# Conformer trunk: sixteen of one channel tile's 31 convolution taps on TensorE instead of all, and four small moves around them

## The chip, the cores and the metric

The kernel runs on one core of a Trainium2 chip. The metric is device time in microseconds (us) of one execution; lower is better. The engines of the core are TensorE (PE, matrix products), VectorE (DVE), ScalarE (ACT), GpSimd (POOL) and SyncE (SP, which issues loads). Each engine works through its own list of instructions in order and waits by semaphores for the others.

## The reference

`x` has 1024 tokens of 1024 channels. There are two layers; each has a token mixer and a SwiGLU feed-forward network of width 2816, both behind an RMS norm, a shift and scale from the conditioning vector `c`, and a gate. Layer 0 mixes tokens by a causal Conformer convolution, layer 1 by trailing means. The change touches the convolution of layer 0 and the norms around it:

```python
def conformer_conv(h, w1, b1, w_dw, b_dw, ln_g, ln_b, w2, b2):
    u = h @ w1 + b1                                # D -> 2D
    a, g = jnp.split(u, 2, axis=-1)
    u = a * jax.nn.sigmoid(g)
    u = lax.conv_general_dilated(                  # depthwise, causal, width 31
        u, w_dw[:, None, :].astype(u.dtype),
        window_strides=(1,), padding=[(CONV_WIDTH - 1, 0)],
        dimension_numbers=("NWC", "WIO", "NWC"),
        feature_group_count=D_MODEL) + b_dw
    u = jax.nn.silu(layer_norm(u, ln_g, ln_b))     # over channels
    return u @ w2 + b2

for i in range(DEPTH):
    mod = c_act @ ada_w[i] + ada_b[i]
    sh_m, sc_m, g_m, sh_f, sc_f, g_f = jnp.split(mod, N_ADA, axis=-1)
    h = modulate(rms_norm(x, norm_mix_g[i]), sh_m, sc_m)
    y = conformer_conv(h, ...) if i % 2 == 0 else multiscale_pool(h, ...)
    x = x + (1.0 + g_m)[:, None, :] * y
    h = modulate(rms_norm(x, norm_ffn_g[i]), sh_f, sc_f)
    y = swiglu_ffn(h, w_gate[i], w_up[i], w_down[i])
    x = x + (1.0 + g_f)[:, None, :] * y
return rms_norm(x, final_g)
```

## The kernel before

**Tiling.** Channels lie on the 128 partitions, so 1024 channels are eight channel tiles (`KT` = 8). Tokens lie along the free dimension in two chunks of 512, A (tokens 0 to 511) and B (512 to 1023). Every operand of a product is split into a high and a low part, and each product of 128x128 by 128x512 is done as three matmuls: high by high, low by high, high by low (`products`, L409). The profile names the high part `hhi`, `uhi`, `vhi` and the low part `hlo`, `ulo`, `vlo`.

**Weights.** `load_weight` (L394) brings a weight tile to `raw` by a DMA on SP's queue. ACT casts it to the high part and writes the negated high part beside it, and a DMA issued from POOL's queue (L403) adds the weight to that, which leaves the low part. Five weight tiles (`W_BUFS`) and three raw ones are in flight.

**Order.** PE's order is the program's own: `units` is a list of pieces of PE work (L1041 to L1077 for this stage), and `run_units` emits them in turn. The work of the other engines is a set of generators, the tasks. `pace` (L178) lets the tasks take steps while the model clock of PE advances, and gives each step to VectorE or GpSimd by their model clocks; `finish` (L190) drives a task to its end. Every matmul goes through one helper and shows as L122, every operation of DVE, ACT and POOL as L100; groups are told apart by their tiles.

**The stage of the change**, in PE's order:

1. `conv_in((A, p))` (L570) for tiles 4 and 5, then 6 and 7 together with B's 6 and 7: for each tile 24 matmuls for `a` and 24 for `g`; `conv_glu` (L562) has ACT take the sigmoid of `g` and DVE form `u`. `u` has 30 columns of halo in front. B's halo is A's last 30 columns, which GpSimd copies to `uhalo` (L568). The first four tiles of A were formed earlier.
2. In between stand the modulation steps: `ada_columns` (L352) loads 512 KB of `ada_w` per step (tile `adaw`, two buffers), PE multiplies it with `c` (group `ada`), and after every eight steps `columns_done` (L375) turns the result around on PE (`adac`), after which DVE adds the bias (`mod<-adac`). The unit `ada_first` starts this task. `norm_first` (L1045) is the task of B's first norm; its sum of squares is in `Squares` (L455): ACT squares a tile, DVE adds it.
3. Three tiles of B (0 to 2), then the taps. Seven of A's eight channel tiles are convolved by `Taps` (L633), whose 31 taps are shared one by one: DVE multiplies and adds into a spare PSUM bank (`ca`), or ACT multiplies (`pr`) and POOL adds (`pa`). At the end DVE adds `pa` to `ca` and does the last tap. Tile 7 is convolved on PE: `split_u` (L597) forms `uhi` and `ulo`, ACT makes a diagonal matrix per tap (`diagonals`, L604: 8 taps per weight buffer, a high and a low part each), and `pe_taps` (L614) runs 31 taps of three matmuls into one bank, `tap`, which ACT takes back to `u`.
4. Two more tiles of B, with the layer norm of A in between (`layer_norm_silu`, L703, a task): DVE sums the eight tiles into `acc` in SBUF, one add as each tile is finished; PE forms the mean over channels; the tiles are centred, squared and summed; PE forms `var` and `rstd`; silu; high and low parts `vhi` and `vlo`.
5. `conv_out` (L739): 192 products `y`. Then the last tile of B and the feed-forward network of A.

PSUM has six banks in turn for results of matmuls (`bank`, L238) and two spare ones for `ca`.

Of the kernel before, what the change touches and what calls it, by code (L numbers as in the profile page):

```python
# [9 lines left out]
F32 = mybir.dt.float32  # L10
F32R = mybir.dt.float32r
# [32 lines left out]

PE_TAPS = (7,)
DIAGS = 8
# [59 lines left out]
def trunk(ctx, tc, xT, c, vec, ada, adan, w1, w2, wgu, wdn, wpl, out):  # L106
# [348 lines left out]
    class Squares:  # L455


        def __init__(self, ch, psum=False):
            self.ch, self.acc, self.psum = ch, None, psum

        def add(self, k):
            ch = self.ch
            if self.acc is None:
                self.acc = bank("acc") if self.psum else temp(ch.n, "acc", 2)
                S_.activation(self.acc, x[ch.i][k], AF.Square)
            else:
                sq = temp(ch.n)
                S_.activation(sq, x[ch.i][k], AF.Square)
                was = self.acc
                if self.psum and k == KT - 1:  # L470
                    self.acc = temp(ch.n, "acc", 2)
                V_.tensor_tensor(self.acc, was, sq, op=ADD)

# [88 lines left out]
    def conv_glu(ch, p, ba, bg):  # L562
        u = st["u", ch.i, p]
        sg = temp(ch.n)
        S_.activation(sg, bg, AF.Sigmoid, bias=V("conv_b1", KT + p))
        V_.scalar_tensor_tensor(u[:, HALO:], ba, V("conv_b1", p), sg, op0=ADD, op1=MUL)
        if ch.i == 0:
            G_.tensor_copy(uhalo[:, p, :], u[:, ch.n : ch.n + HALO])  # L568

    def conv_in(*todo):  # L570

        def emit(take):
            got = {}
            for each in todo:
# [14 lines left out]
                conv_glu(ch, p, *b)  # L589
                if ch.i == 0 and p in PE_TAPS:  # L590
                    split_u(p)
                elif ch.i == 0:
                    T["taps", 0, p] = Taps(A, p)
        tiles = list(dict.fromkeys(e[1] for e in todo if e))
# [9 lines left out]
    def diagonals(p, js):  # L604

        def make():
            wt = wts.tile([P, 2, D], F32R, tag="w", name=nm("diag"))
            for i, j in enumerate(js):
                for part, w in enumerate((vecs[:, _COLS["conv_wdw"] + j * KT + p :][:, :1], wlow[:, j, p - PE_TAPS[0] : p - PE_TAPS[0] + 1])):
                    S_.activation(wt[:, part, i * P : i * P + P], ident, AF.Copy, scale=w)  # L610
            return wt
        return make

    def pe_taps(p):  # L614

        groups = [range(j, min(j + DIAGS, CW)) for j in range(0, CW, DIAGS)]
        us = []
        for i, js in enumerate(groups):
            def emit(take, i=i, js=js):
# [3 lines left out]
                for q, j in enumerate(js):  # L623
                    products(b, wt, q, [v[:, j : j + A.n] for v in st["us", p]], j == 0, j == CW - 1)
                    if q % 4 == 3:
                        pace()
                if i == len(groups) - 1:
                    S_.activation(st["u", 0, p][:, HALO:], b, AF.Identity, bias=V("conv_bdw", p))
                    st["taps", 0][p] = True
            us.append((emit, diagonals(p, js)))  # L630
        return us

    class Taps:  # L633
# [4 lines left out]

        def __init__(self, ch, p):
            self.ch, self.p, self.done, self.urgent = ch, p, False, False  # L640
            self.next, self.acc, self.part, self.busy = 0, None, None, 0
            tasks.append(self)

        def step(self, e):
# [6 lines left out]
            if self.next < CW - 1:  # L651
# [27 lines left out]
                return True  # L679
            if e != "V":  # L680
                return False
            if self.part is not None:
                V_.tensor_tensor(self.acc, self.part, self.acc, op=ADD)
# [313 lines left out]

    wdw = V("conv_wdw", 0, CW * KT).rearrange("p (j k) -> p j k", k=KT)[:, :, PE_TAPS[0] : PE_TAPS[-1] + 1]
    whigh = cst.tile([P, CW, len(PE_TAPS)], F32R, name="whigh")
    wlow = cst.tile([P, CW, len(PE_TAPS)], F32, name="wlow")  # L1000
    S_.copy(whigh, wdw)
# [171 lines left out]
```

## Time and profile before

| | |
|---|---|
| Median of three runs | 1880.17 us (1877.83 to 1882.66) |
| The profiled run | 1878.38 us, of which the span of the profile 1876.6 us |
| PE busy | 1821.7 us, 97% of the span |
| DVE, ACT, POOL busy | 971.8, 984.5, 622.2 us |
| Mean granted PE clock | 0.989 of full speed |
| DMA | 382.31 MB at 204 GB/s |

The times of single instructions, of stages and of waits come from the one profiled execution, the median from separate runs; the profiled run was 1.8 us below the median. In the tables of groups a row reads: line, engine, operation, out<-in, partitions x elements, count | busy time in us, mean ns of one | idle time of the engine just before them and who ended it. In order of time it reads: start, length, engine, line, operation, out<-in, count, and in brackets the idle time before.

### The profile page before, as it was taken

To read this page: it belongs to the slowest core of one execution; us is meant where nothing else is said; L and a number is where in the kernel's file an instruction comes from. 1 tells how busy PE (TensorE), PEld (TensorE's weight loads), DVE (VectorE), ACT (ScalarE), POOL (GpSimd) and SP (SyncE) were. 2 spreads that over 40 slices of the span, in tenths; PEclk is the share of its full clock that TensorE was granted. 3 is DMA by queue.
4 is the path that set the end of the run, shared out by engine and by line. 5 is a ranking of instruction groups with operands and counts; after the bars stand their busy time and mean duration, and the time that the engine had idled before them with its cause. 6 is when DMAs were issued, how large, how long until landed. Compare 5 with 4: busy or idle time off the path is not lost.

```text
span 1876.6 us, 22033 instructions
## 1 busy us (share of the span) xinstructions
PE 1821.7 (97%) x8197; PEld 1481.9 (79%) x8197; DVE 971.8 (52%) x1489; ACT 984.5 (52%) x1304; POOL 622.2 (33%) x668
## 2 busy tenths in 40 slices
PE   6899999999999999999999999999999999999996
PEld 4676678888888887888888888888888888888886
DVE  7699743998876235486533223644432233323225
ACT  3577756866756454554553445645534454443443
POOL 3488621787753211273211111421111111111111
PEclk9999989999999999999999999999999999999998
DMA  8968558899897986999887887878878879788882
GB/s 265 298 185 233 155 114 202 207 230 218 213 233 186 239 217 165 261 266 291 231 204 181 200 197 179 196 180 208 185 181 199 198 174 247 180 206 187 193 185 61
DMA packets 115292, 382.31 MB, mean 204 GB/s; under 512 B 11889, under 2 KB 22257, under 8 KB 115186
## 3 DMA queue, kind: packets, MB, share of 16 engines
q0 software_dynamic: 43488, 158.35, 46.2%
q1 hardware_dynamic: 70544, 221.51, 34.8%
q8 instruction: 64, 1.05, 0.2%
q10 hardware_dynamic: 1154, 1.05, 0.2%
q14 instruction: 42, 0.34, 0.0%
HBM read 376.67 MB, written 4.19 MB: 203 GB/s over the span
## 4 chain that ended last, share of the span: by engine, by line
PE 91%; DVE 4%; DMA 3%; ACT 0%; issue 0%; POOL 0%; SPq 0%; DVEq 0%; ACTq 0%; POOLq 0%
PE dn L122 25%; PE gate L122 25%; PE up L122 24%; PE y L122 6%; PE a L122 3%; PE g L122 3%; PE first L122 2%; DMA adaw<-in_adan_dram 2%; DVE t L100 1%; PE ada L122 1%; PE tap L122 1%; DVE x L100 1%; DVE adaw L100 1%; PE var L122 1%; DMA w<-in_wdn_dram 1%; DVE acc L100 1%
## 5 line engine op out<-in xcount | busy, mean ns | idle before, releaser
L100 ACT CAST w<-raw 128x1024 fp32r<-128x1024 f32 x312 | 326.0, 1045 | 514.8 <-issue 294.4
L122 PE MATMUL dn<-ghi,w 128*128 128x512 f32 (+1 forms) x1440 | 450.0, 389 | 2.2 <-ACT ghi L100 1.2
L122 PE MATMUL up<-hhi,w 128*128 128x512 f32 x1408 | 451.4, 390 | 0.0
L122 PE MATMUL gate<-hhi,w 128*128 128x512 f32 x1408 | 450.9, 390 | 0.0
L403 POOL DMA_DIRECT2D w<-in_wgu_dram x176 | 154.2, 876 | 767.6 <-ACT w L100 750.1
L100 DVE SCALAR_TENSOR_TENSOR x<-dn,gains,x 128x512 f32<-128x512 f32 (+1 forms) x360 | 261.8, 735 | 122.1 <-PE dn L122 121.7
L122 PEld LDWEIGHTS dn<-ghi,w 128*128 128x128 f32 x1440 | 270.4, 189 | 62.0 <-ACT ghi L100 1.6
L100 ACT ACTIVATE w<-raw 128x1024 fp32r<-128x1024 f32 x302 | 318.9, 1056 | 0.0
L100 DVE TENSOR_TENSOR t<-t,up 128x512 f32<-128x512 f32 x88 | 60.4, 686 | 492.4 <-PE up L122 472.0
L122 PEld LDWEIGHTS gate<-hhi,w 128*128 128x128 f32 x1408 | 264.3, 188 | 55.4
L122 PEld LDWEIGHTS up<-hhi,w 128*128 128x128 f32 x1408 | 264.3, 188 | 54.7
L122 PE MATMUL dn<-glo,w 128*128 128x512 f32 (+1 forms) x720 | 280.7, 390 | 1.6 <-POOL glo L100 1.6
L122 PE MATMUL gate<-hlo,w 128*128 128x512 f32 x704 | 274.3, 390 | 1.5 <-DVE hlo L100 1.5
L122 PE MATMUL up<-hlo,w 128*128 128x512 f32 x704 | 273.9, 389 | 0.0
L100 POOL TENSOR_TENSOR pa<-pa,pr 128x512 f32<-128x512 f32 x165 | 231.0, 1486 | 23.0 <-ACT pr L100 20.3
L100 DVE SCALAR_TENSOR_TENSOR ca<-u,vecs,ca 128x512 f32<-128x512 f32 x255 | 176.2, 746 | 0.7
L122 PEld LDWEIGHTS dn<-glo,w 128*128 128x128 f32 x720 | 136.6, 190 | 30.3 <-POOL glo L100 1.9
L122 PEld LDWEIGHTS gate<-hlo,w 128*128 128x128 f32 x704 | 132.1, 188 | 29.8 <-DVE hlo L100 2.3
L122 PEld LDWEIGHTS up<-hlo,w 128*128 128x128 f32 x704 | 132.2, 188 | 27.2
L403 POOL DMA_DIRECT2D w<-in_wdn_dram x88 | 77.9, 885 | 226.5 <-ACT w L100 224.4
L100 ACT ACTIVATE t<-gate 128x512 f32<-128x512 f32 x88 | 52.3, 594 | 161.0 <-PE gate L122 154.4
L100 DVE SCALAR_TENSOR_TENSOR adaw<-adaw,cact 128x1024 f32<-128x1024 f32 x64 | 106.2, 1660 | 36.0 <-DMA adaw<-in_ada_dram 35.8
(134 smaller groups left out, 1792.3 us busy)
## 6 DMA issues: line engine op xcount, KB each, us to landing
raw<-in_wgu_dram SPq DMA_DIRECT2D x176, 512.0 KB, 7.2
w<-in_wgu_dram POOLq DMA_DIRECT2D x176, 512.0 KB, 8.0
raw<-in_wdn_dram SPq DMA_DIRECT2D x88, 512.0 KB, 5.4
w<-in_wdn_dram POOLq DMA_DIRECT2D x88, 512.0 KB, 9.1
adaw<-in_ada_dram SPq DMA_DIRECT2D x48, 512.0 KB, 7.8
raw<-in_w_dram SPq DMA_DIRECT2D x44, 512.0 KB, 6.2
w<-in_w_dram POOLq DMA_DIRECT2D x34, 512.0 KB, 8.1
adaw<-in_adan_dram SPq DMA_DIRECT2D x32, 512.0 KB, 5.3
```

The source lines that it names most:

```text
L100: self.last = self.order(getattr(self.eng, name)(out, *args, **kw))
L122: last_mm[0] = nc.tensor.matmul(out, lhsT, rhs, start=start, stop=stop).ins.name
L403: order(nc.gpsimd.dma_start(low if len(src.shape) == 2 else low.rearrange("p (a b) -> p a b", a=src.shape[1]), src, accum_op=ADD))
```

## The change

Five edits:

- **Taps.** `PE_TILE, PE_TAPS = 7, 16`: PE does taps 0 to 15 of tile 7, two buffers of diagonals instead of four. The other 15 taps become a `Taps` task that begins at tap 16. It may end only when the PE part is there: ACT copies the bank to SBUF (`ny`, held as `other`), and DVE adds it to `ca`. `whigh` and `wlow` shrink to 16 columns.
- **Halo copies.** The eight copies of A's last 30 columns go from GpSimd to DVE.
- **Squares.** `Squares` is split into `square` and `sum`; B's first norm issues the square of tile k ahead of the sum of tile k - 1.
- **The mean's sums.** For chunk A all sums but the last go to a PSUM bank instead of SBUF; for B the first goes to SBUF and the later ones are in place as before.
- **Modulation.** The unit `ada_first` moves from ahead of tile 4 to behind it, and the unit that finishes the modulation moves from behind the taps to behind the two tiles of B that follow them.

```diff
-PE_TAPS = (7,)
+PE_TILE, PE_TAPS = 7, 16
...
-            self.ch, self.acc, self.psum = ch, None, psum
+            self.ch, self.acc, self.psum, self.waiting = ch, None, psum, []
...
+        def square(self, k):
+            ch = self.ch
+            if k == 0:
+                self.acc = sq = bank("acc") if self.psum else temp(ch.n, "acc", 2)
+            else:
+                sq = temp(ch.n)
+                self.waiting.append(sq)
+            S_.activation(sq, x[ch.i][k], AF.Square)
+        def sum(self, last):
+            was = self.acc
+            if self.psum and last:
+                self.acc = temp(self.ch.n, "acc", 2)
+            V_.tensor_tensor(self.acc, was, self.waiting.pop(0), op=ADD)
+        def add(self, k):
+            self.square(k)
+            if k:
+                self.sum(k == KT - 1)
...
-            G_.tensor_copy(uhalo[:, p, :], u[:, ch.n : ch.n + HALO])
+            V_.tensor_copy(uhalo[:, p, :], u[:, ch.n : ch.n + HALO])
...
-                if ch.i == 0 and p in PE_TAPS:
-                    split_u(p)
-                elif ch.i == 0:
-                    T["taps", 0, p] = Taps(A, p)
+                if ch.i == 0:
+                    T["taps", 0, p] = Taps(A, p, PE_TAPS if p == PE_TILE else 0)
+                    if p == PE_TILE:
+                        split_u(p)
...
-        groups = [range(j, min(j + DIAGS, CW)) for j in range(0, CW, DIAGS)]
+        groups = [range(j, min(j + DIAGS, PE_TAPS)) for j in range(0, PE_TAPS, DIAGS)]
...
-                    S_.activation(st["u", 0, p][:, HALO:], b, AF.Identity, bias=V("conv_bdw", p))
-                    st["taps", 0][p] = True
+                    T["taps", 0, p].other = temp(A.n, "ny", 2)
+                    S_.copy(T["taps", 0, p].other, b)
...
-        def __init__(self, ch, p):
+        def __init__(self, ch, p, first=0):
-            self.next, self.acc, self.part, self.busy = 0, None, None, 0
+            self.next, self.acc, self.part, self.other = first, None, None, None
+            self.awaits = first > 0
...
-            if e != "V":
+            if e != "V" or self.awaits and self.other is None:
                 return False
+            if self.other is not None:
+                V_.tensor_tensor(self.acc, self.other, self.acc, op=ADD)
             if self.part is not None:
                 V_.tensor_tensor(self.acc, self.part, self.acc, op=ADD)
...
-        acc = temp(n, "acc", 2)
+        acc = None
         for k in range(1, KT):
             while not (st["taps", ch.i][k - 1] and st["taps", ch.i][k]):
                 yield "wait"
-            V_.tensor_tensor(acc, vs[0] if k == 1 else acc, vs[k], op=ADD)
+            was = vs[0] if k == 1 else acc
+            if k == KT - 1 or ch.i and acc is None:
+                acc = temp(n, "acc", 2)
+            elif acc is None:
+                acc = bank("acc")
+            V_.tensor_tensor(acc, was, vs[k], op=ADD)
...
-    unit(ada_first)
     def norm_first():
         squares = Squares(B, True)
-        for k in range(KT):
-            squares.add(k)
+        for k in range(KT + 1):
+            if k < KT:
+                squares.square(k)
+            if k > 1:
+                squares.sum(k == KT)
             yield
...
         conv_in((A, p))
+        if p == FIRST:
+            unit(ada_first)
...
-    for p in PE_TAPS:
-        for u in pe_taps(p):
-            unit(*u)
+    for u in pe_taps(PE_TILE):
+        unit(*u)
     unit(lambda take: held.__setitem__(0, True))
-    unit(lambda take: finish(T["ada", 0]))
-    unit(lambda take: finish(*(T["taps", 0, p] for p in range(KT) if p not in PE_TAPS)))
+    unit(lambda take: finish(*(T["taps", 0, p] for p in range(KT))))
     for p in rest[len(rest) - HOLD - HOLD_LN : len(rest) - HOLD]:
         conv_in((B, p))
+    unit(lambda take: finish(T["ada", 0]))
     need("ln_a")
```

More of the change, by code (lines that the diff above doesn't have):

```diff
@@ L608, in make @@
             for i, j in enumerate(js):
-                for part, w in enumerate((vecs[:, _COLS["conv_wdw"] + j * KT + p :][:, :1], wlow[:, j, p - PE_TAPS[0] : p - PE_TAPS[0] + 1])):
+                for part, w in enumerate((vecs[:, _COLS["conv_wdw"] + j * KT + p :][:, :1], wlow[:, j : j + 1])):
                     S_.activation(wt[:, part, i * P : i * P + P], ident, AF.Copy, scale=w)
@@ L623, in emit @@
                 for q, j in enumerate(js):
-                    products(b, wt, q, [v[:, j : j + A.n] for v in st["us", p]], j == 0, j == CW - 1)
+                    products(b, wt, q, [v[:, j : j + A.n] for v in st["us", p]], j == 0, j == PE_TAPS - 1)
                     if q % 4 == 3:
@@ L996, in trunk @@
             wt = load_weight(w1k[k], 2 * FIRST * P, load_next)
-    wdw = V("conv_wdw", 0, CW * KT).rearrange("p (j k) -> p j k", k=KT)[:, :, PE_TAPS[0] : PE_TAPS[-1] + 1]
-    whigh = cst.tile([P, CW, len(PE_TAPS)], F32R, name="whigh")
-    wlow = cst.tile([P, CW, len(PE_TAPS)], F32, name="wlow")
+    wdw = V("conv_wdw", 0, CW * KT).rearrange("p (j k) -> p j k", k=KT)[:, :PE_TAPS, PE_TILE]
+    whigh = cst.tile([P, PE_TAPS], F32R, name="whigh")
+    wlow = cst.tile([P, PE_TAPS], F32, name="wlow")
     S_.copy(whigh, wdw)
```

9 lines of the change are left out of this document (removed).

## The prediction

> **What bounds the kernel now.** I read the busy shares on the page first, then the chain that ended last.
>
> ```profile
> PE 1821.7 (97%) x8197; PEld 1481.9 (79%) x8197; DVE 971.8 (52%) x1489; ACT 984.5 (52%) x1304; POOL 622.2 (33%) x668
> PE 91%; DVE 4%; DMA 3%; ACT 0%; issue 0%; POOL 0%; SPq 0%; DVEq 0%; ACTq 0%; POOLq 0%
> ```
>
> TensorE is busy for 97% and carries 91% of the chain. A saving must therefore take work from PE or shorten one of its few gaps. The change touches only the stage from chunk A's fifth convolution tile to the first matmul of chunk A's output convolution. I cut that stage at four points: the first matmul of tile 4 (70.73), the first tap (204.56), the end of the taps (231.50) and the first `y` matmul (268.94). In each row come the window's length, the busy time and count of PE, PEld, DVE, ACT and POOL, the granted clock, the DMA share and GB/s.
>
> ```profile
> 70.73:92.50 21.77, 15.23 (x73) 10.06 (x71) 11.44 (x17) 13.46 (x20) 9.51 (x12) 0.84 0.99 264
> 92.50:204.56 112.06, 109.42 (x605) 77.18 (x605) 103.18 (x153) 84.16 (x158) 87.56 (x84) 1.00 0.67 189
> 204.56:231.50 26.94, 25.74 (x137) 17.82 (x133) 19.56 (x26) 17.05 (x24) 21.25 (x19) 1.00 0.77 215
> 231.50:268.94 37.44, 30.53 (x119) 24.48 (x119) 21.36 (x44) 23.62 (x32) 12.83 (x14) 0.82 0.51 112
> 340.00:700.00 360.00, 360.00 (x1591) 297.04 (x1590) 250.32 (x350) 227.19 (x298) 197.28 (x178) 1.00 0.88 219
> ```
>
> From 340 on PE has no gap at all, so what the stage gains before `y` should arrive at the end. Inside the stage PE idles 21.77 - 15.23 = 6.5 us and 112.06 - 109.42 = 2.6 us, 9.2 together ahead of the taps. In the second window DVE is busy for 103 of 112 us: it is nearly as full as PE.
>
> The waits of PE and its order of time say what those gaps are (time, length, group, in brackets the wait and who ended it).
>
> ```profile
> 86.62 1.08 PE L122 MATMUL ada<-adaw,ccols 128*32 128x256 f32 x8 [5.97 <-DMA adaw<-in_adan_dram]
> 204.56 0.50 PE L122 MATMUL tap<-uhi,diag 128*128 128x512 f32 x1
> 207.54 0.64 PE L122 MATMUL ada<-adaw,ccols 128*32 128x256 f32 x8
> 208.11 0.50 PE L122 MATMUL tap<-uhi,diag 128*128 128x512 f32 x1
> 236.20 2.08 PE L122 MATMUL mean<-acc,ones 128*128 128x512 f32 x2 [4.66 <-DVE acc L100]
> 238.07 0.85 PE L122 MATMUL adac<-quarters,t 128*128 128x4 f32 x4
> 247.56 1.86 PE L122 MATMUL var<-ones,acc 128*128 128x1 f32 x8 [2.25 <-DVE acc L100]
> 254.41 1.05 PE L122 MATMUL rstd<-ident,col 128*128 128x128 f32 x8
> 258.23 5.44 PE a L122 x24
> 268.94 0.39 PE L122 MATMUL y<-vhi,w 128*128 128x512 f32 x1
> ```
>
> The first gap waits 5.97 us for a modulation load. The mean of the layer norm waits 4.66 us for the vector engines' sum, and the variance 2.25 us. A full-width matmul costs 5.44/24 = 0.2267 us, and a modulation step of eight small matmuls about 0.7 us (0.57 from its start to the next tap, and the refill).
>
> **The change, first: PE ahead of the taps.** In the compiled order of the changed kernel, 24 modulation steps instead of 28, and two `adac` groups instead of three, stand before the first tap. That is 4 x 0.7 + 0.4 = 3.2 us moved back, not saved. The first modulation loads are now issued behind two more raw weight loads, so the 5.97 us wait should go, and PE reach its clock sooner than the 0.84 of that window. In return tile B0's gate matmuls now wait for a `mod` of DVE, and the first tap for the sigmoid of B1, behind two weight casts on ACT. What this leaves of the 9.2 us is bounded by nothing recovered (a DMA queue at 0.99 must still carry every byte) and by the 9.2 plus about 2 of clock. I take 7, near the upper end, because one named wait makes up most of it. First tap: 204.56 - 3.2 - 7 = 194.4.
>
> **Second: 45 fewer tap matmuls, and what replaces them.** 45 x 0.2267 = 10.2 us leave PE. From the first tap PE has 48 matmuls (10.9), an `adac` and two steps (1.8) to the last tap: 207.1. Three steps and twelve matmuls later (4.8) it is at the mean, near 212. But the mean needs all eight tiles summed, and that goes by the vector engines.
>
> ```profile
> L100 POOL TENSOR_TENSOR pa<-pa,pr 128x512 f32<-128x512 f32 x75 | 100.6, 1433 | 17.0 <-ACT pr L100 16.1
> L100 DVE SCALAR_TENSOR_TENSOR ca<-u,vecs,ca 128x512 f32<-128x512 f32 x121 | 83.7, 746 | 0.6
> L100 DVE SCALAR_TENSOR_TENSOR u<-u,vecs,ca 128x512 f32<-128x512 f32 x7 | 5.1, 742 | 0.2
> L100 ACT CAST w<-raw 128x1024 fp32r<-128x1024 f32 x21 | 21.9, 1045 | 24.0 <-PE g L122 12.1 <-PE tap L122 6.6 <-PE a L122 5.3
> L403 POOL DMA_DIRECT2D w<-in_w_dram x20 | 18.5, 924 | 26.1 <-ACT w L100 23.5 <-issue 2.2 <-POOL pa L100 0.4
> 182.87 13.25 DVE L100 SCALAR_TENSOR_TENSOR ca<-u,vecs,ca 128x512 f32<-128x512 f32 x20
> 208.76 5.32 POOL L100 TENSOR_TENSOR pa<-pa,pr 128x512 f32<-128x512 f32 x4
> 231.58 0.69 ACT L100 ACTIVATE u<-tap,vecs 128x512 f32<-128x512 f32 x1 [2.00 <-PE tap L122]
> 233.07 0.70 DVE L100 TENSOR_TENSOR ca<-pa,ca 128x512 f32<-128x512 f32 x1 [6.87 <-POOL pa L100]
> ```
>
> Already now the mean comes 3 us after POOL's last partial sum (233.07), whose lateness DVE spent 6.87 us waiting for. The change gives these engines the tile's other 15 taps: DVE one start and five `ca` operations, POOL one start and seven adds, one more join each of `pa` and of the PE part, one more closing operation. Two chains end at the mean:
>
> DVE: the third `mod` waits for the `adac` that stands twelve matmuls into the taps, 194.4 + 2.8 = 197.2. Behind it, up to the mean, stand 38 operations at about 0.68 (13.25/20 = 0.66 in a run of `ca`, 0.74 for the closing one): 26 us. With 2 us for a sigmoid that one of them awaits: 225.
>
> POOL: the issue of one weight load stands behind two casts on ACT, which stand behind the copy of the PE part, which needs the last tap. So 207.1 + 0.69 + 2 x 1.05 + 0.9 = 210.8; then ten adds at 5.32/4 = 1.33 (13.3) and four DVE operations (2.75): 226.9. If POOL is late for that issue, the sum moves with it: it keeps most of its 9.85 us gap below and the gaps for `pr`, and I allow 5 us, 232.
>
> ```profile
> 94.33 0.89 POOL L403 DMA_DIRECT2D w<-in_w_dram  x1 [9.85 <-ACT w L100]
> L100 POOL COPY uhalo<-u 128x30 f32<-128x30 f32 x8 | 2.0, 244 | 12.5 <-DVE u L100 12.5
> L100 DVE TENSOR_TENSOR mod<-adac,vecs 128x8 f32<-128x8 f32 x4 | 0.6, 157 | 1.8 <-PE adac L122 1.8
> ```
>
> A bound from below is DVE without a gap. Up to the mean it is busy now for 11.44 + 103.18 + 19.56 us and the last 3; fourteen operations more at 0.68 make it 146.7, and 70.73 + 146.7 = 217, later than PE's 212. I take the mean at 228 (bounds 217, and 248, the slow rival below): the 16 us or so that PE waits there are the price of the edit, and larger than the 4.66 of now.
>
> **Third: mean to `y`.** Now 32.74 us: 108 matmuls, mean, `adac`, var, rstd, and the 2.25 wait. In the changed order stand 84 matmuls (19.0), four steps (2.8), mean (1.9), var (1.9) and rstd (1.1), 26.7. Ahead of var are 36 matmuls and four steps instead of 24 matmuls, so its wait shrinks; with 0.5 for it and 0.8 for a clock that drops after the long gap, 28. `y` starts at 256 instead of 268.94: 13 earlier.
>
> **Edits costed at nothing.** The eight halo copies leave POOL (244 ns each; in the rows by operation, from 66 to 270, POOL stood 12.5 us ahead of them) and go to DVE. No row shows one there: between 0.157 (a 128x8 operation) and that plus an add of 1.43 that holds it up, 1.3 to 12.7 us for eight. I take the low end, since all stand before the `adac` wait, in a window that leaves DVE 112.06 - 103.18 = 8.9 us idle; uncovered, each microsecond delays the mean by one. ACT loses 30 diagonals and gains seven `pr`; two more function tables are loaded, 1.3 us each, under its waits; uncovered one would cost 1.3.
>
> ```profile
> L100 ACT ACTIVATE diag<-ident,vecs 128x128 fp32r<-128x128 f32 x31 | 12.1, 390 | 0.5 <-PE a L122 0.5
> L100 ACT ACTIVATE pr<-u,vecs 128x512 f32<-128x512 f32 x75 | 50.7, 715 | 10.0 <-POOL pa L100 8.5 <-DVE hlo L100 1.0 <-DVE u L100 0.2
> L100 ACT ACT_TABLE_LOAD x3 | 3.8, 1283 | 2.7 <-PE first L122 2.6
> L100 DVE TENSOR_TENSOR acc<-acc,u 128x512 f32<-128x512 f32 x6 | 11.1, 1857 | 0.2
> L100 DVE TENSOR_TENSOR acc<-acc,t 128x512 f32<-128x512 f32 x14 | 9.8, 697 | 11.1 <-ACT t L100 10.3
> ```
>
> Issuing the squares ahead aims at the 10.3 us that the sums of squares waited for `t`; they are off PE's path as long as B's norm is ready for its first matmuls, as it is now. The mean's sums in a PSUM bank may bring `acc<-acc,u` from 1.86 us to the 0.70 of `acc<-acc,t`: six of them, but five run as their tiles finish; the last stays in SBUF. That is up to 1 us inside the four operations above.
>
> One page speaks against the copies. The Trainium skill, "SBUF — State Buffer", section "SBUF: two separate sides", says that VectorE and GpSimd share a port pair as an exclusive lock, which a plain fp32 copy from SBUF to SBUF, or an operation with two SBUF inputs, must hold alone. The 1857 ns of `acc<-acc,u` against 697 fit it. By that rule a copy waits out a GpSimd add, the upper end above, and the saving would be some 4 to 8 us less.
>
> **The rivals.**
> (1) The waits inside the vector chains vanish, and DVE's bare work sets the mean at 217: `y` at 245, 24 us earlier, 1878.4 - 24 + 1.8 = 1856. For it: POOL is busy only 97 of the 134 us before the taps. Against: in the page's rows 6.87 us of DVE already wait for POOL.
> (2) The gaps before the taps stay, as a DMA queue at 0.99 suggests, or come back as the two new waits. Everything behind is 7 us later: 6 saved, 1874. Against: the 5.97 us wait has one named load behind it.
> (3) The halo copies on DVE are held up by POOL's adds, 11.4 us beyond the low price, of which 3 to 7 us find slack. The mean comes 4 to 8 us later: 1871 to 1875. For it: the 1857 against 697; against: `ca` at 746 beside running adds.
> (4) Slower: POOL's queue sets the end. Its last partial sum is at 233.07 now. Seven adds and a start more, less the copies, are 9.3 + 0.7 - 2.0 = 8; the weight load's issue, which now stands behind the PE part's copy, adds up to 3.7. If the tap stage starts no earlier, the mean comes at 233.1 + 8 + 3.1 = 244 to 248 and `y` at 272 to 276: 1883 to 1887. It decides from the point where the mean is later than 241 (268.94 - 28). For it: POOL's 21.25 of 26.94 in the tap window; against: POOL waits 17.0 us for `pr` and 26.1 for casts, gaps that an earlier PE shortens.
>
> **How the numbers follow.** The sum stands against the profiled run: span 1876.6, run 1878.4, 1.8 below the median of the runs. Forecast 1878.4 - 13 + 1.8 = 1867. Chances: forecast 0.54, rivals 0.08, 0.15, 0.10 and 0.13 in this order. The range 1857 to 1880 takes in the mean between about 218 and 241 and leaves out rival 1 and most of 4. A measurement of this kernel can tell 0.3%, 5.6 us. Faster than that: nearly all of the forecast, rival 1, half of 2 and most of 3, 0.75; slower: most of 4, 0.10; the rest 0.15. The likeliest case alone: 1861 to 1872.
>
> **What would show it.** First tap near 194, no wait of 6 us for the first modulation load; last tap near 207; a wait of some 16 us at the mean, released by `acc` of DVE; the mean near 228; `y` near 256, and the same 13 us at the end. Wrong: a mean at 218 or before (rival 1), a first tap after 200 (2), halo copies above 0.5 us (3), the mean after 241 (4), or a gap behind `y` that gives the gain back.

## The result, and the profile after

The changed kernel is slower by 0.6%. Its median is 1892.26 us (1887.36 to 1894.59, six runs) against 1881.22 for the kernel before in the same comparison; the ratio is 1.0061, with a 95% interval of 1.0043 to 1.0079. The forecast was 1867. The profiled run took 1891.55, its span 1889.8, 13.2 more than before.

The stage of the change, cut at its first matmul, at 106 (behind the last of the early gaps), at the first tap, at the end of the taps, at the first `y` and at the end of chunk A's `y`. In each row come the length, the busy time and count of PE, PEld, DVE, ACT and POOL, the granted clock, the DMA share and GB/s:

```profile
70.56:106.00 35.44, 27.63 (x139) 20.43 (x138) 25.26 (x41) 28.52 (x40) 23.28 (x22) 0.97 0.96 262
106.00:209.19 103.19, 98.05 (x512) 68.46 (x511) 91.49 (x132) 65.52 (x114) 76.41 (x71) 0.96 0.63 178
209.19:222.50 13.31, 13.31 (x73) 9.53 (x75) 12.09 (x19) 9.86 (x13) 11.35 (x13) 1.00 0.95 225
222.50:270.58 48.08, 33.81 (x162) 22.95 (x163) 34.26 (x62) 28.41 (x38) 22.82 (x22) 0.82 0.50 129
270.58:322.50 51.92, 46.17 (x197) 37.91 (x196) 13.67 (x22) 29.64 (x40) 11.31 (x13) 0.93 0.76 167
```

The tap run is as short as forecast, 13.3 us instead of 27. But it begins at 209.19, not at 194 (before: 204.56): ahead of it PE idles 7.8 us in the first row and 5.1 in the second, 13.0 together, where it idled 9.2. The `y` block, for which no change was forecast, takes 51.9 us; before it took 43.5. Set against the kernel before, the 13.2 us of the two spans are 4.6 up to the first tap, 3.0 gained from there to `y`, 8.4 lost in `y` and 3.1 lost behind it.

The lines of PE in order of time that matter (start, length, operation, count, and the wait before it):

```profile
84.40 0.73 PE L123 MATMUL a<-hhi,w 128*128 128x512 f32 x2 [2.35 <-DMA w<-in_w_dram]
95.61 0.64 PE L123 MATMUL ada<-adaw,ccols 128*32 128x256 f32 x8 [1.61 <-DMA adaw<-in_adan_dram]
103.06 0.64 PE L123 MATMUL ada<-adaw,ccols 128*32 128x256 f32 x8 [3.86 <-DMA adaw<-in_adan_dram]
209.19 0.39 PE L123 MATMUL tap<-uhi,diag 128*128 128x512 f32 x1
228.46 1.08 PE L123 MATMUL ada<-adaw,ccols 128*32 128x256 f32 x8 [5.40 <-DMA adaw<-in_adan_dram]
242.39 2.04 PE L123 MATMUL mean<-acc,ones 128*128 128x512 f32 x2 [8.06 <-DVE acc L101]
270.58 0.39 PE L123 MATMUL y<-vhi,w 128*128 128x512 f32 x1
287.38 1.02 PE L123 MATMUL adac<-quarters,t 128*128 128x4 f32 x4 [5.75 <-ACT t L101]
```

The one wait of 6 us is gone, and three others, 7.8 us together, stand in its place, in a row with DMA at 0.96. Then the mean comes at 242.39, 33.2 us behind the first tap (forecast 33.6), and `y` comes 28.2 behind the mean (forecast 28). And in the middle of `y` an `adac` waits 5.75 us for ACT. What ACT does just before, in the same view:

```profile
285.92 0.62 ACT L101 ACTIVATE acc<-x 128x512 f32<-128x512 f32 x1
286.44 0.62 ACT L101 ACTIVATE t<-x 128x512 f32<-128x512 f32 x1
286.96 0.36 ACT L101 COPY t<-ada 128x256 f32<-128x256 f32 x1
```

ACT copies the modulation row behind the output of two `y` tiles, four halves of weights and two squares; PE needs the copy at once, having just finished the same two tiles. So the last modulation columns were held back: the kernel's own rule (`held`, `held_back`) lets the columns that are not done when the taps end wait until two of the eight `y` tiles are through. Before, the columns were done in time and the rule never acted.

The chain to the mean, on POOL and DVE:

```profile
225.43 0.88 POOL L404 DMA_DIRECT2D w<-in_w_dram  x1 [0.45 <-ACT w L101]
226.04 12.99 POOL L101 TENSOR_TENSOR pa<-pa,pr 128x512 f32<-128x512 f32 x10
...
225.44 10.10 DVE L101 SCALAR_TENSOR_TENSOR ca<-u,vecs,ca 128x512 f32<-128x512 f32 x15
235.64 0.70 DVE L101 TENSOR_TENSOR ca<-ny,ca 128x512 f32<-128x512 f32 x1
237.85 0.70 DVE L101 TENSOR_TENSOR ca<-pa,ca 128x512 f32<-128x512 f32 x1 [1.51 <-POOL pa L101]
```

This is POOL's chain of the forecast, operation by operation: last tap, PE part, weight load issued, ten adds, the join. POOL's last sum ends at 239.0, 6 us later than before (233.0). Counted from the first tap the chain is as long as forecast; against the forecast it is late because the first tap is.

### The profile page after: what moved, and what is told of

Read it like the earlier page. It is cut to its first block, busy times and chain, and to the rows that moved or that the text cites. A ratio compares the mean times of both kernels' runs of the same rounds, so it can differ in the third digit from the quotient of the medians.

```text
span 1889.8 us, 21953 instructions
## 1 busy us (share of the span) xinstructions
PE 1816.7 (96%) x8152; PEld 1475.7 (78%) x8152; DVE 986.0 (52%) x1506; ACT 982.9 (52%) x1283; POOL 630.3 (33%) x668
## 4 chain that ended last, share of the span: by engine, by line
PE 87%; DVE 5%; DMA 5%; issue 1%; ACT 1%; POOL 1%; SPq 0%; DVEq 0%; ACTq 0%; POOLq 0%
PE dn L123 24%; PE gate L123 24%; PE up L123 23%; PE y L123 6%; PE a L123 2%; PE g L123 2%; PE first L123 2%; DMA adaw<-in_adan_dram 2%; DMA adaw<-in_ada_dram 2%; DVE t L101 1%; DVE adaw L101 1%; DVE x L101 1%; PE ada L123 1%; DVE hlo L101 1%; PE tap L123 1%
## 5 line engine op out<-in xcount | busy, mean ns | idle before, releaser
L123 PE MATMUL up<-hlo,w 128*128 128x512 f32 x704 | 273.9, 389 | 0.0
L101 POOL TENSOR_TENSOR pa<-pa,pr 128x512 f32<-128x512 f32 x172 | 241.9, 1511 | 31.9 <-ACT pr L101 29.0
L101 DVE SCALAR_TENSOR_TENSOR ca<-u,vecs,ca 128x512 f32<-128x512 f32 x260 | 180.4, 749 | 0.9
L101 ACT ACTIVATE pr<-u,vecs 128x512 f32<-128x512 f32 x172 | 115.3, 715 | 27.5 <-DVE u L101 12.0
```

The costliest lines, as they stand in the source:

```text
L101: self.last = self.order(getattr(self.eng, name)(out, *args, **kw))
L123: last_mm[0] = nc.tensor.matmul(out, lhsT, rhs, start=start, stop=stop).ins.name
```

## The experiments

All ratios are against the kernel before, run on the same chip in the same comparison. "Alone" means the kernel before with that edit as its only one. Where one kernel is set against another, the ratios' difference is taken and given in us of 1880. The times inside the stage (first tap, mean, `y`) come from one profiled execution of each kernel. From the last `y` matmul to the end of the span these executions take 1560.5 to 1567.5 us, so a few us gained or lost inside the stage need not show in the whole time, and the reverse.

### What each edit is worth in the changed kernel

The modulation's start put back:

```diff
+    unit(ada_first)
     def norm_first():
...
-        if p == FIRST:
-            unit(ada_first)
```

> The changed kernel with the modulation started ahead of tile 4 again, as before the change; all other edits stay. Theory M (the move of the modulation makes PE late: B's variance stands behind a modulation step whose load comes late, and DVE then idles for var and rstd): DVE's waits for var and rstd of B's norm (4.7 and 4.8 us) shrink to under 2 us together, the first tap comes at 199 to 204 instead of 209, the mean follows it by some 33 us as in the changed kernel, and the time is 5 to 10 us below the changed kernel's 1892, that is 1882 to 1887. Theory V (the vector engines' 15 more taps and the halo copies make everything late): first tap at 207 or later, time within 3 us of 1892.

1888.50, ratio 1.0045 (1.0031 to 1.0059), first tap at 211.2, mean at 244.1. Theory M falls in the very place it was made for: the tap did not come earlier. DVE's wait for var stayed (5.0 us), only that for rstd went.

No columns held back:

```diff
-            if k == KT - 1 and (j == 2 or not held[0]):
+            if k == KT - 1:
                 yield from columns_done(j, acc)
-            elif k == KT - 1:
-                held_back.append((j, acc))
```

> The changed kernel, but the last modulation columns are turned around as soon as they are done instead of being held until two of the eight y tiles are through. Theory H (PE stands 5.75 us inside y for ACT's copy of the modulation row, and runs slowly after it): no wait for adac, y 43.5 to 44 us from first to last matmul instead of 52, first tap, mean and first y matmul unchanged within 1 us, time 7 to 9 us below the changed kernel's, that is 1883 to 1885. Rival: the gap only moves, to the place where adac now stands ahead of var or to the first gate matmul; time within 3 us of 1892.

1883.76, ratio 1.0022 (1.0010 to 1.0034): 7.3 us less than the changed kernel by the ratios, 8.5 by the medians. The chain that ended last shows `y` in one piece again:

```profile
274.03 43.52 PE y L123 x192
```

In the changed kernel the same view had it in two, with 7.4 us between the end of the first and the start of the second:

```profile
270.75 10.21 PE y L123 x45
288.40 34.30 PE y L123 x144
```

Mean (244.1) and `y` (273.9) were no earlier than in the changed kernel; in this execution they were 1.7 and 3.3 later, more than the 1 us expected. The held columns are a cost by themselves.

All 31 taps on PE again, with the other four edits:

```diff
-PE_TILE, PE_TAPS = 7, 16
+PE_TILE, PE_TAPS = 7, 31
...
-                    T["taps", 0, p] = Taps(A, p, PE_TAPS if p == PE_TILE else 0)
                     if p == PE_TILE:
                         split_u(p)
+                    else:
+                        T["taps", 0, p] = Taps(A, p)
```

> The changed kernel with all 31 taps of tile 7 on PE again; the other four edits stay. Theory M: the first tap is still late, 207 to 210, since the load of the vector engines is not its cause; the mean wait shrinks to under 5 us, the mean comes at 238 to 243, no earlier than in the changed kernel by more than 5 us; time 1888 to 1895. Theory V: with 15 taps fewer on DVE and POOL the first tap comes at 200 to 204, and the time returns to 1878 to 1884.

1894.10, ratio 1.0070 (1.0055 to 1.0084), first tap at 210.2. The 15 taps on the vector engines are not what makes the first tap late: theory V falls too. The mean comes at 243.6, 1.2 later than in the changed kernel, although PE does 27 us of taps before it instead of 13. The columns were held back here too (`y` took 51.9 us).

The halo copies on POOL again, the other edits left:

> The changed kernel with the eight halo copies on POOL again. In the changed kernel they took 5.5 us on DVE (median 0.18, longest 2.25). If they are what makes DVE late (a part of theory V), first tap and mean come 4 to 5 us earlier and the time is 1886 to 1889. If not (theory M), DVE's gain is used up by POOL's waits for u (12.5 us ahead of the copies before the change), and the time is 1890 to 1896.

1894.91, ratio 1.0080 (1.0063 to 1.0096). No gain; the first tap was at 208.7, the mean at 248.3.

So only one of the four gave back much. No single edit held the late first tap, and the edits were tried the other way round.

### Each edit alone

```diff
-            G_.tensor_copy(uhalo[:, p, :], u[:, ch.n : ch.n + HALO])
+            V_.tensor_copy(uhalo[:, p, :], u[:, ch.n : ch.n + HALO])
```

> The kernel before, with the eight halo copies on DVE as its only edit. PE's order is that of before up to the mean. Theory S (the first tap is late in every variant so far, at 209 to 211 against 204.6, because the early stage, in which DMA is busy 0.9 or more, is run in another order: here the first weight DMAs leave POOL's queue 3 us later): first tap at 207 to 211, time 1882 to 1888. Rival (only several edits together make the tap late): first tap at 203 to 206, time within 3 us of 1880.

1883.80, ratio 1.0018 (1.0006 to 1.0031). First tap at 215.6, the latest of all, with PE's order up to there that of before. The copies as groups (count | busy, mean ns): here, then in the changed kernel

```profile
L101 DVE COPY uhalo<-u 128x30 f32<-128x30 f32 x8 | 10.2, 1278 | 0.1
```

```profile
L101 DVE COPY uhalo<-u 128x30 f32<-128x30 f32 x8 | 5.5, 682 | 0.1
```

The shortest of them took 0.17 us. The mean price lies between the ends of the forecast, alone near the upper one.

The squares ahead alone (this edit and the next two are those parts of the change):

> The kernel before, with the squares issued one ahead of the sums as its only edit. Theory S: DVE's wait of 8.75 us for a square shrinks, but PE is held by the modulation loads as before, so the first tap stays at 203 to 206 and the time within 3 us of 1880. Rival (the squares take ACT's time from the weight casts, whose loads and modulation loads then come later): first tap at 207 to 211, time 1883 to 1888.

1879.59, ratio 0.9998 (0.9981 to 1.0015): nothing, though the first tap came at 207.6 and the mean at 239.3 in the profiled execution, 3 us later than before. A first tap that is 3 us late thus need not make the kernel slower.

The modulation moved alone, start and end as in the change:

> The kernel before, with the modulation moved as its only edit (start behind tile 4, end behind the two later tiles of B). Two steps fewer stand before the first tap, the other work of PE is that of before. If the move gains what it was forecast to (most of 9.2 us of gaps): first tap at 194 to 199 and time 1873 to 1877. Theory S (the bytes of the early stage bound it, whatever comes first): gaps before the first tap of 8 to 13 us, first tap at 202 to 208, time 1878 to 1886.

1873.02, ratio 0.9956 (0.9941 to 0.9972): faster, by 8 us. The time is that of the first expectation, the first tap that of the second: 204.6, as before, behind gaps of 8.6 us. The gain lies behind it:

```profile
234.39 1.65 PE L123 MATMUL mean<-acc,ones 128*128 128x512 f32 x2 [2.17 <-DVE acc L101]
```

The mean came 1.8 us earlier and `y` 28.5 behind it, where it was 32.7: `y` began at 262.9, 6.0 earlier. The windows from the mean (in the second row from the last tap, 2.2 us of waiting earlier) to `y`, before and here:

```profile
236.20:268.94 32.74, 30.49 (x118) 24.48 (x119) 18.52 (x40) 21.04 (x29) 10.44 (x10) 0.83 0.45 103
```

```profile
232.20:262.90 30.70, 26.95 (x120) 21.67 (x120) 18.48 (x39) 22.50 (x29) 8.86 (x11) 0.94 0.58 120
```

The matmuls of B between the two are 96 in both. The gap ahead of the mean fell from 4.66 to 2.17 us, and the granted clock behind it rose from 0.83 to 0.94: PE is busy 3.5 us less for the same matmuls of B.

The shorter tap run alone, with no columns held back, since by the program's order the shorter run would bring that rule into play:

> The kernel before, with the shorter tap run on PE and the modulation columns never held back; halo copies on POOL, squares, sums and the modulation's start as before. PE's order is that of before up to the taps, so the first tap comes at 203 to 206; if the vector engines' chain then needs the 33 us that it took in the changed kernel, the mean comes at 237 to 240, y at 262 to 266, and the time is 3 to 7 us below before: 1873 to 1877. Theory V (15 more taps on DVE and POOL make even the first tap late): first tap after 207, time 1879 to 1885.

1879.55, ratio 0.9994 (0.9979 to 1.0009), against 1873 to 1877 expected. 45 matmuls left PE and next to nothing came of it. The mean was at 242.9, 6.7 later than before, waited for by 5.7 us. PE's order has 24 more matmuls of B ahead of the mean here, so `y` still began at 266.5, 2.4 us earlier than before. But `y` waited too, and took 47.4 us instead of 43.5 (two lines in order of time, then the window of `y`):

```profile
266.53 0.50 PE L123 MATMUL y<-vhi,w 128*128 128x512 f32 x1 [2.54 <-DVE vhi L101]
267.90 0.79 PE L123 MATMUL y<-vlo,w 128*128 128x512 f32 x1 [0.86 <-POOL vlo L101]
266.53:313.92 47.39, 46.53 (x192) 38.01 (x192) 14.30 (x21) 29.00 (x39) 12.27 (x12) 0.93 0.70 160
```

So PE stood waiting for the vector engines at both ends of the layer norm, and its clock in `y` was 0.93 instead of 1.00.

Alone, then, the edits come to about -8 (modulation), +3 (halo copies), 0 (squares), -1 (taps, less than its interval) and +8 (held columns); the sums were tried with the modulation only, below, and gave 0. The held columns' share was measured in the changed kernel. That is +2 in all, where the change costs 11. The rest arises between them.

### Pairs with the moved modulation

> The kernel before with the modulation moved and the halo copies on DVE, no columns held back. Alone the move of the modulation gained 7.8 us and the halo copies cost 3. Theory L (the copies on DVE wait for POOL's adds and spoil the move's gain: DVE is late for B's norm and for the mean): copies of 5 us or more in all on DVE, first tap at 208 or later, mean at 239 or later, time 1879 to 1887. Rival (the two add up, the loss of the change came with the taps): first tap at 203 to 207, time 1874 to 1878.

1886.65, ratio 1.0033 (1.0019 to 1.0047): 14 us above the modulation alone, with the rule for held columns taken out, as in all runs below except those with the sums and the squares. The time is in the range of theory L. PE's waits (total, count, longest):

```profile
PE ada L123 <- DMA adaw<-in_adan_dram: 11.9, 6, 4.1
PE mean L123 <- DVE acc L101: 9.6, 1, 9.6
PE a L123 <- DMA w<-in_w_dram: 2.5, 1, 2.5
```

> The kernel before with the modulation moved and 16 taps on PE, no columns held back. If the shorter tap run is worth nothing because the vector engines' chain sets the mean (the mean was waited for by 2.2 us with the modulation moved alone): first tap at 203 to 206, mean at 235 to 240, wait there of 8 us or more, time within 3 us of the modulation alone, 1870 to 1877. If the vector engines still have room: mean at 228 to 232 and 1864 to 1869.

1883.74, ratio 1.0012 (0.9997 to 1.0027): 11 us above the modulation alone. Mean at 247.1 with a wait of 10.85: worse than the expectation for vector engines that set the end. DVE and POOL on the way to it:

```profile
211.42 5.38 DVE L101 TENSOR_TENSOR acc<-acc,u 128x512 f32<-128x512 f32 x1
...
238.70 0.87 POOL L402 DMA_DIRECT2D w<-in_w_dram  x1 [6.82 <-ACT w L101]
239.31 4.24 POOL L101 TENSOR_TENSOR pa<-pa,pr 128x512 f32<-128x512 f32 x3
...
243.58 0.69 DVE L101 TENSOR_TENSOR ca<-pa,ca 128x512 f32<-128x512 f32 x1 [3.05 <-POOL pa L101]
```

POOL stands 6.8 us at a weight load's issue with three adds behind it, and one sum of two SBUF tiles takes 5.38 us on DVE. What PE was relieved of became the chain that PE waits for. From the first tap to `y` the kernel before takes 64.4 us, the modulation alone 58.3, the shorter tap run alone 59.0, and both together 63.8: what each of the two gains there is lost when both are done. `y` took 47.4 us here as well.

> The kernel before with the modulation moved and the mean's sums in PSUM. The sums come down from 1.25 us to 0.70 each, two of them stand on the chain to the mean: 1 us or a little more earlier, time 1870 to 1873. If PE's own work sets the mean already: no change, 1873.

1873.49, ratio 0.9959 (0.9943 to 0.9975), against 0.9956 without: nothing more, though the sums came down to 0.695 us each, on average.

> The kernel before with the modulation moved and the squares one ahead. DVE waited 7.5 us for B's variance with the modulation moved alone, so squares that come earlier cannot start it earlier: no change, 1870 to 1876. If the squares on ACT delay weight casts: first gap on a weight load, first tap later by 2 us or more, 1875 to 1879.

1875.29, ratio 0.9975 (0.9961 to 0.9988): within the interval of the modulation alone, if anything worse.

### How the halo copies undo the gain

The copies on DVE, not told to the planner, so that PE's order stays that of the modulation alone; then the copies on ACT, told:

```diff
-            V_.tensor_copy(uhalo[:, p, :], u[:, ch.n : ch.n + HALO])
+            order(nc.vector.tensor_copy(uhalo[:, p, :], u[:, ch.n : ch.n + HALO]))
```

```diff
-            V_.tensor_copy(uhalo[:, p, :], u[:, ch.n : ch.n + HALO])
+            S_.copy(uhalo[:, p, :], u[:, ch.n : ch.n + HALO])
```

> The modulation moved and the halo copies on DVE, but the planner is not told of the copies: PE's order and the count of POOL's adds (76 up to the mean, against 79 with copies that it counts) are those of the modulation alone, so that only the copies themselves change. Theory L (the copies wait for POOL's adds on DVE): copies of 5 us or more in all, mean at 239 or later, time 1878 to 1885. Rival P (the copies are cheap; the planner, which counts them, gives POOL three more adds and PE another order): mean at 233 to 239, time 1871 to 1876.

> The modulation moved and the halo copies on ACT, no columns held back. PE's order is that of the kernel with the copies on DVE (1886.7), POOL has 76 adds. Theory L: free of DVE and POOL, the copies cost nothing there: mean at 233 to 239, time 1871 to 1876. Rival P, as far as PE's order and POOL's order around the first weight loads are what costs: 1881 to 1887.

Uncounted on DVE: 1879.43, ratio 0.9995 (0.9979 to 1.0011), 3.3 us of copies. On ACT: 1885.26, ratio 1.0025 (1.0014 to 1.0036), 1.7 us of copies, none of them longer than 0.22. So the price of the copies on DVE is not the reason: moved to ACT they undo the gain as well as on DVE (1.0033). About half of it (0.9995 against 1.0033) comes from the other orders that the planner gives when it counts them. The other half is there with PE's order kept. Every run without copies on POOL has one mark in common, and the next runs try whether it is the cause. POOL's first operations of the stage, in the changed kernel:

```profile
69.60 0.70 POOL L101 TENSOR_SCALAR pa<-u,vecs 128x512 f32<-128x512 f32 x1 [7.85 <-DVE u L101]
75.45 1.96 POOL L404 DMA_DIRECT2D w<-in_w_dram  x2 [5.16 <-ACT pr L101]
```

Before, the first weight load went out at 71.99, behind two halo copies. Now it goes out at 75.45, and PE meets its first wait for a weight at 84.40. The last thing that this load waits for by the program, ACT's half of the weight, was done at 71.2; the `pr` that the view names is read by a later add.

> The changed kernel with two edits: no columns held back (alone worth 8.5 us, 1883.8) and the halo copies on ACT instead of DVE. If the copies on DVE are what is left of the loss: mean 3 us or more earlier than 244 and 1876 to 1880. If the 15 taps on DVE and POOL are (as with the modulation alone, where they cost 10.7): mean at 243 or later, 1881 to 1886.

1882.59, ratio 1.0015 (0.9997 to 1.0034), mean at 241.0 with a wait of 11.75, first weight load at 75.6: not to be told from the same kernel with the copies on DVE (1.0022).

The copies split between POOL and DVE, tiles 0 to 3 on POOL, and the other way round; PE's order is the same in both:

```diff
+            if p < FIRST:
+                G_.tensor_copy(uhalo[:, p, :], u[:, ch.n : ch.n + HALO])
+            else:
+                order(nc.vector.tensor_copy(uhalo[:, p, :], u[:, ch.n : ch.n + HALO]))
```

> The modulation moved; the halo copies of tiles 0 to 3 on POOL, those of tiles 4 to 7 on DVE and not counted by the planner. PE's order is that of the modulation alone. Theory Q (what the copies' absence on POOL costs is the start of POOL's first weight DMA: it came at 72 to 74 in every run with copies ahead of it on POOL and at 75.3 to 76.6 in every run without, although all that it waits for was done at 71 to 72): first weight DMA at 72 to 74, no wait of PE for a weight near 85, time 1870 to 1875. Rival L (DVE's later copies, which wait for POOL's adds, are what costs): 1877 to 1882.

> The mirror image: the copies of tiles 0 to 3 on DVE, not counted, and those of tiles 4 to 7 on POOL. Theory Q: first weight DMA at 75 to 77, a wait of PE of 2 to 3 us for a weight near 85, time 1877 to 1882, as with all eight on DVE. Rival L: 1870 to 1875.

POOL in order of time, first four on POOL, then last four on POOL:

```profile
71.84 0.21 POOL L101 COPY uhalo<-u 128x30 f32<-128x30 f32 x1 [0.64 <-DVE u L101]
72.58 1.04 POOL L402 DMA_DIRECT2D w<-in_w_dram  x1 [0.54 <-issue]
```

```profile
71.49 0.70 POOL L101 TENSOR_SCALAR pa<-u,vecs 128x512 f32<-128x512 f32 x1 [7.45 <-DVE u L101]
77.21 1.04 POOL L402 DMA_DIRECT2D w<-in_w_dram  x1 [5.02 <-ACT t L101]
```

First four on POOL: 1870.95, ratio 0.9946 (0.9929 to 0.9964), not to be told from the modulation alone (0.9956), although its four copies on DVE took 1.7 us each. Last four on POOL: 1875.31, ratio 0.9974 (0.9957 to 0.9991), with a wait for a weight of 2.48 at 86.4, although its copies on DVE took 0.27 each. That is the opposite of theory L. The times differ by 4 to 5 us, with intervals that overlap a little, but the late first load does not account for them. In the profiled executions the two kernels reach the first tap (206.4 and 206.2), the mean (236.3 and 236.2) and `y` together, and the whole `y` block is the same in the chain that ended last, first four on POOL, then last four:

```profile
264.77 43.52 PE y L123 x192
264.94 43.52 PE y L123 x192
```

The 4.0 us between the two spans arise only behind 700 us. So theory Q is not borne out inside the stage: a late first load and PE's wait for it were made up before the first tap. With all eight copies on DVE and the same order of PE, `y` ended 7.5 us later than in either split. Why it takes the loss of both halves was not found.

> The changed kernel, all five edits, with no columns held back (1883.8 so far) and the first four halo copies back on POOL. If the late first DMA is worth the 6 us that it costs beside the modulation alone: 1876 to 1880. If the vector engines, which have 15 taps more, set the mean anyway: mean at 242 or later and 1881 to 1885.

1889.27, ratio 1.0051 (1.0034 to 1.0067), mean at 250.9 with a wait of 12.83. The first load is in time, there are no held columns, and the kernel is slower than with late loads (1.0022). What holds the mean is seen on POOL and DVE:

```profile
240.56 0.87 POOL L402 DMA_DIRECT2D w<-in_w_dram  x1 [8.68 <-ACT w L101]
241.16 6.41 POOL L101 TENSOR_TENSOR pa<-pa,pr 128x512 f32<-128x512 f32 x5
246.40 0.70 DVE L101 TENSOR_TENSOR ca<-pa,ca 128x512 f32<-128x512 f32 x1 [13.27 <-POOL pa L101]
```

POOL's last adds stand in its list behind a weight load that waits for ACT's casts, and ACT in turn waits 7.7 us for PE. The same is seen with the moved modulation and the shorter run (6.82 us, three adds) and in the changed kernel with the copies back on POOL (7.53 us, three adds). These three have the latest means of all, 247 to 251. In the changed kernel the load waits 0.45 us and the ten adds follow it, and the mean is at 242. With 15 more taps on DVE and POOL the mean is late in any order tried, 241 to 251; but it came at 242 to 245 in five runs with all 31 taps on PE as well.

## Why the prediction was wrong

**First step: failed.** "I take 7" of 9.2 us of gaps plus clock, "because one named wait makes up most of it". Nothing was recovered: 13.0 us of gaps instead of 2.2, and the first tap at 209.2 instead of 194.4, 14.8 us later than forecast. Of these, 10.8 are gaps. The rest is PE's busy time ahead of the taps, which was to fall by 3.2 us and rose by 1.0, although three steps (27 to 24; the prediction counted 28 before) and an `adac` were moved away. The row for it stood in the prediction, DMA at 0.99 in that window; the bound "a DMA queue at 0.99 must still carry every byte" was the value to take. With the modulation moved alone, one gap of 6.92 at 98.9 takes the place of the one of 5.97 at 86.6. In the changed kernel it is split into three, and the clock from 99 to 118 is 0.81 to 0.84. This step is the whole of the saving that is missing at `y`: 14.8 us late at the first tap, 14.6 late at `y`. That DMA's bytes set these gaps fits the rows and was not shown by a run of its own.

**Second and third step: right in size.** First tap to mean 33.2 (33.6), mean to `y` 28.2 (28), with POOL's chain last as named. But the wait at the mean is only 8.1, not 16: PE came to it 7.5 us later after the first tap than forecast, 5.4 of them lost at a modulation load that the prediction did not have. In the other kernels with 16 taps on PE the mean came 33 to 43 us behind the first tap, by the order in which the engines' lists happen to stand. The 108 matmuls that the prediction counted between mean and `y` before are 96; what it put down to the other twelve, 2.7 us, was the slow clock behind the gap, 0.83 in that window.

**What was not costed: the held columns.** That an `adac` stood inside `y` was to be seen in the compiled order, and the prediction gave it no price. It is worth 7 to 9 us, shown by leaving the rule out, and is the largest single loss. The waits of a moved or late step should be looked up on every engine, and ACT's queue ahead of this copy is the row that was missing.

**Edits costed at nothing.** Squares and sums: right, no effect alone or with the modulation moved. Halo copies: wrong. They cost 3 us alone, and 7 to 14 with the modulation moved; in the changed kernel, putting them back on POOL gave nothing (1.0080). The price was looked for on the engine that takes them. Half of what they cost beside the modulation lies in the planner's order; the cause of the other half is open, since neither the copies' length nor POOL's late first load explains it.

**The rivals.** The slow one had the place and the point right: the mean at 242.4, behind POOL's last sum (226.04 + 12.99 = 239.0; before 233.0), past its mark of 241, though short of its 244. By its own sum that gives 1882 (a mean at 242.4 and 28 more, 1.5 past the old `y`); the held columns make most of the other 10. Rival 2 (gaps stay) happened as well, and given together with the other it ends on the slow side; they had been priced as if one excluded the other. Rival 3 named the lock: copies were held up as priced, but the two splits of the copies go against it as the cause of the time.

**Why 45 matmuls off PE bought nothing** is seen in the taps alone (0.9994). The mean was waited for by 4.66 us already before, so vector work set its time. With 15 taps more on DVE and POOL the vector work ends 6.7 us later; `y` begins 2.4 us earlier all the same, waits for DVE and POOL at its start, and runs 4 us longer. A busy share of 97% is the share of all stages; in this one PE was not the last.

What stays open: why the shorter tap run costs 11 us beside the moved modulation and nothing without it. The slow sum is not needed for it: with all five edits and the first four copies on POOL every sum took about 0.70 us, and the mean was the latest of all. POOL's wait at the weight load is there in each of the three runs with the latest means, and it is the nearest reading, but no run moved that load alone.

## What to carry to other kernels

Before work is moved off the busiest engine, look at which engine ends the stage: if the busiest engine already waits for others there, moving its work to them makes that wait longer. A gap at a transfer in a window where DMA is nearly full may only move: here 5.97 us at one modulation load became 6.92 at another, or three waits of 7.8 together. Before work is given to an engine, look in that engine's list for a load that must wait with the work behind it. Where orders come from a planner, test every edit alone and in pairs: here one edit was worth 8 us and the five together cost 11.

## What the runs showed of the hardware

**One DVE operation with two SBUF inputs lasted as long as a run of GpSimd adds.** In the changed kernel, in order of time on DVE and on POOL:

```profile
148.76 5.39 DVE L101 TENSOR_TENSOR ulo<-u,uhi 128x542 fp32r<-128x542 f32 x1
...
148.30 5.27 POOL L101 TENSOR_TENSOR pa<-pa,pr 128x512 f32<-128x512 f32 x4
```

In several other runs the same operation took 0.70 to 0.75 us. Here it ends 0.6 us after the fourth add, and not after the first; the sum of 5.38 us above ended 0.6 us after the last of three adds. The Trainium skill, "SBUF — State Buffer", section "SBUF: two separate sides", speaks of a lock for one whole instruction; the trace agrees that the two hold each other up, but the loser waited for the whole run of adds. Sums into PSUM with one SBUF input stayed at 0.69 to 0.70 in all eight runs that have them.

**A pause of POOL that no wait explains.** In the ten runs without a copy on POOL ahead of it, the first weight load went out 75.3 to 77.2 us into the span, with its waits done some 4 us earlier. The table of DMA queues of the changed kernel has 42 transfers of the instruction kind on queue 14, of 8 KB each:

```profile
q14 instruction: 42, 0.34, 0.0%
```

In each of the ten runs the DMA records show two of them in that pause, and the load starts 1.73 to 1.76 us after the start of the second. With copies there, one such transfer is seen, and the load goes out at 72 to 74. That POOL waited for its code there is the nearest reading, and was not shown by itself; nor did the pause cost time inside the stage where it was tried alone, with the last four copies on POOL. The Trainium skill, "Runtime: NRT & Kernel Launch", section "Instruction fetch mechanics", calls the cost of such a fetch mostly hidden; if it is one, POOL's 4 us of pause were not hidden from POOL here, in a window with DMA at 0.96.
